# A hybrid decoder layer: decay rows masked on GpSimd, weights and sums loaded in another order, the causal mask as fp32r tiles

## The chip, the cores and the metric

One core of one Trainium2 chip runs the whole program. The metric is the device time of one execution in microseconds (us). The engines are named as the profile names them: PE is TensorE's matmul, PEld its weight load, DVE is VectorE, ACT is ScalarE, POOL is GpSimd, SP issues most of the DMAs.

## The reference

One decoder layer on 1024 tokens of width 1024, all in float32. One projection of the normed input feeds two groups of heads: a differential attention of 4 heads and a gated delta rule of 4 heads, whose outputs are put side by side, projected, and added to the input; an MLP with a squared ReLU of width 4096 follows.

```python
h = rms_norm(x, norm1_w[l])
proj = h @ w_in[l]
...
# group A, per block of 128 queries
s = jnp.where(causal, s, jnp.finfo(jnp.float32).min)
p = jax.nn.softmax(s, axis=-1)
a = p[:, :, 0] - lam * p[:, :, 1]
...
# group B, in chunks of 64
decay = jnp.where(tri, jnp.exp(jnp.where(tri, gdiff, 0.0)), 0.0)
Lmat = jnp.where(strict, jnp.einsum('bhncd,bhnjd->bhncj', k_beta, k) * decay, 0.0)
qk = jnp.where(tri, jnp.einsum('bhncd,bhnjd->bhncj', q, k) * decay, 0.0)
...
x = x + mix @ w_out[l]
h = rms_norm(x, norm2_w[l])
x = x + jnp.square(jax.nn.relu(h @ w_up[l])) @ w_down[l]
```

## The kernel before, in words

Every large product is made of three matmuls: an operand is split into a part rounded to fp32r (suffix H, a cast on ACT) and the rest (suffix L, a subtraction on DVE), and H*H, H*L and L*H are added up in PSUM. So each block of weights goes DMA, ACT cast, DVE subtraction, PE. `load_unit` (L182) does it for the projections, with `wraw` for the raw block and `wH`, `wL` for the parts; `split` (L1298) does it for the MLP.

The kernel has these stages, in order of time:

- **Norm and first columns** (L333 to L390; the order on PE, DVE and ACT is written by hand). For each tile of 128 tokens the input is squared on ACT, scaled on DVE into `hn` (`z_norm`, L328), transposed on PE (L235) and multiplied with two blocks of columns, whose halves `z_round` and `z_rest` make.
- **The delta group's projection** (L512 to L676; the order on all engines comes from a scheduler). `dn_units` makes six blocks of 256 columns, each in four half heads of 24 matmuls into one of two PSUM banks (`ps_dn`). ACT copies the bank to `cp` (L525), and ACT and DVE run a convolution (`cy`, L527 to L529) and make keys, queries and values. `keys` and `queries` transpose them (`ps_t`), multiply them with each other (`ps_m`), and multiply the product with a decay matrix (L633, L656). The decay of head h lies in `dts[h]` (tile `dtm`, 128x1024): `decay_rows` (L576) fills it with the mask `after` (0 where a later token looks at an earlier one, -1e30 elsewhere), which a DMA on SP's queue spreads from SBUF over the eight blocks of the row (L578), and adds the running sums `cgr_d` with a second DMA on GpSimd's queue that accumulates (L579). `decay` (L581) then takes the exponential on ACT (L585). A small inverse (`invert`, L596) runs on DVE beside it, and results are parked in DRAM (`park`, L549).
- **Scan, attention and output projection** (L698 to L1441). PE's order is written by a planner, `Interleave`: streams of work hand it their next piece with a due time worked out from estimated durations, and it takes the first stream, by priority, whose due time has come. `horner` (L712) finishes the inverse, `scan` (L764) runs over 8 chunks with the state `St`, `da_units` (L918) makes the other projection (`ps_qk`), `leave` norms it and `da_turns` (L891) transposes it (`ps_qkt`), `scores` (L1022) makes softmax maps, `values` (L1101) their products, `outproj` (L1200) the output projection and the second norm (`norm2`, L1224). The causal mask of a diagonal block is added by a matmul of a bf16 identity with a bf16 mask (L1079). DVE, ACT, POOL and SP are ordered by the scheduler.
- **MLP** (L1442 to L1725). Up and down projections each take seven products of blocks for eight (sums and differences of operands, as in Strassen's scheme). `down` (L1661) takes two halves of operands, splits them (`split4`), runs 96 matmuls into four PSUM banks, and adds these to the sums `accs`, which come back from DRAM by `load_acc` (L1653). `both` (L1703) makes the differences of weights on DVE, 128x2048 at a time. On PE the order is that of the code, on the other engines the scheduler's.

DMAs on SP's queue are issued in order; each issue that waits holds those behind it.

Of the kernel before, what the change touches and what calls it, by code (L numbers as in the profile page):

```python
# [18 lines left out]
P = 128  # L19
# [97 lines left out]
def tile_hymba_layer(  # L117
# [215 lines left out]
    with tc.manual_schedule(engines={T.engine, V.engine, S.engine}):  # L333
# [47 lines left out]
        z_norm(2)  # L381
        z_gate(0, 1, banks0[1])
        for tb in range(1, NT):
            for u in range(2):
# [3 lines left out]
                if u == 0 and tb + 1 < NT:  # L388
# [5 lines left out]
    identb = const.tile([P, P], BF16, name="identb")  # L394
    V.tensor_copy(identb, ident)
# [3 lines left out]
    caus_f = n1.tile([P, P], F32, name="caus_f")  # L399
    G.memset(caus_f, 0.0)  # L400
    G.affine_select(caus_f, caus_f, pattern=[[-1, P]], compare_op=ALU.is_ge, fill=-1.0e30,
                    base=0, channel_multiplier=1)
    caus = const.tile([P, P], BF16, name="caus")
    V.tensor_copy(caus, caus_f)
# [52 lines left out]
    u, au, e, w1, lw, d1, z1 = (n32(n) for n in ("gu", "gau", "gte", "gw1", "glw", "gd1", "gz1"))  # L457
    V.tensor_tensor(hc(u), av, dtb.unsqueeze(2).broadcast_to([P, 4, 8]), ALU.add)
    V.scalar_tensor_tensor(au, u, -1.0, u, ALU.mult, ALU.max)
    S.activation(e, au, AF.Exp, scale=-1.0)  # L460
# [87 lines left out]

    def park(h, hf, slot, src):  # L549
        nc.sync.dma_start(park_d[h, 4 * hf:4 * hf + 4, :, slot, :].rearrange("c p d -> p c d"), v4(src))  # L550
# [25 lines left out]
    def decay_rows(h):  # L576
        dts[h] = sa.tile([P, SEQ], F32, tag="dtm", name="dtm", bufs=4)
        nc.sync.dma_start(v4(dts[h]), after.unsqueeze(1).broadcast_to([P, NT, P]))  # L578
        G.dma_start(dts[h], cgr_d[h * SEQ:(h + 1) * SEQ].partition_broadcast(P), accum_op=ALU.add)  # L579
# [7 lines left out]
    for h in range(HEADS):  # L587
        decay_rows(h)
# [80 lines left out]
    for n, (kind, h, hf, o) in enumerate(skew(dn_units())):  # L669
        (queries, keys, values_in)[kind](h, hf, o)  # L670
        for _ in range(0 if n < 12 else 2 if n < 16 else 4):
            next(inverse, None)
        if n == 22:
            first_w = load_unit(w_in_v, [(512, 256), (0, 256)], 0, 4, eng=V, rp=sf)
    for _ in inverse:
        pass  # L676

# [15 lines left out]
    sd = sdctx.enter_context(tc.tile_pool(name="sd", bufs=1, **right))  # L693
    px = qctx.enter_context(tc.tile_pool(name="px", bufs=2, space=PSUM, **right))
# [17 lines left out]
    def horner():  # L712
# [13 lines left out]
        at = [flow.now + 5000] * HEADS  # L726
# [164 lines left out]
    def da_turns():  # L891
        for i in range(4 * NT):
# [3 lines left out]
            r = yield from flow.bank("px", at=max(t + 500, qa_free[i % 2] - 500))  # L896
# [21 lines left out]
    def da_units():  # L918
# [5 lines left out]
        w = [(first_w, [0.0] * 4), half_w(w_in_v, todo[0], 4)]  # L924
# [97 lines left out]
    def scores():  # L1022
# [6 lines left out]
        for u, (h, tb) in enumerate(order):  # L1029
# [34 lines left out]
            for m in range(2):  # L1064
# [7 lines left out]
                for pc in range(npc):  # L1072
# [5 lines left out]
                    if last:  # L1078
                        T.matmul(sc[:, 512 * pc + pl - P:512 * pc + pl], identb, caus, start=False, stop=True)  # L1079
# [120 lines left out]
    def outproj():  # L1200
# [23 lines left out]
        def norm2(tb, pos):  # L1224
# [10 lines left out]
            for i in range(2):  # L1235
                sl = slice(512 * i, 512 * i + 512)
                if i == 0 or pos >= 4:
                    normed_by[:] = [V.scalar_tensor_tensor(hn[i], accs[tb][:, sl], r, w2b[:, sl], ALU.mult, ALU.mult)]
                else:
                    S.activation(hn[i], accs[tb][:, sl], AF.Copy, scale=r)  # L1240
                    G.tensor_tensor(hn[i], hn[i], w2b[:, sl], ALU.mult)
            t = flow.chain(act(512, True), act(512, True), vec(1), vec(1), powr(1))
            if pos >= 4:
                return hn, flow.chain(vec(512, 60), vec(512, 60), start=t - flow.HOP)
            flow.chain(vec(512, 60), start=t - flow.HOP)
            t = flow.chain(act(512), ("G", 1230.0), start=t - flow.HOP)
            return hn, t
# [170 lines left out]
    def read_first():  # L1418
        a0 = pools["uz"].tile([P, 2, 512], F32, tag="ua0", name="ua0")
        S.copy(a0, banks["X0"])  # L1420
        V.tensor_tensor(a0, a0, banks["Y"], ALU.add)
        act2(a0)
        nc.sync.dma_start(ud[1][0], a0)
        u[0] = {"a": a0}

# [90 lines left out]
    held(1, [0, 1])  # L1516
    held(2, [0, 1])
# [3 lines left out]
    held(1, [2])  # L1521
    rest(0, 5)
    held(1, [3])
    read_first()
# [95 lines left out]
    bankA = [X[0][:, 0], X[0][:, 1]] + Z  # L1620
# [32 lines left out]
    def load_acc():  # L1653
# [102 lines left out]
```

## Time and profile before

| | us |
|---|---|
| median of 3 runs | 1261.04 (1260.59 to 1262.15) |
| the profiled execution | 1260.75 |
| its span, first to last instruction | 1259.0 |
| PE busy | 1226.7 |
| DVE busy | 834.3 |
| ACT busy | 614.9 |
| POOL busy | 147.1 |
| mean granted clock of TensorE | 0.996 |

A row of the view by group has the line, the engine, the operation, out<-in and the shapes, the count, then the busy time and the mean of one in ns, then the engine's idle time ahead of these instructions and what ended it. In the timeline a row has start, duration, engine, line, operation and count; idle time ahead of it stands in brackets with what ended it. The view by windows gives the busy time of PE, PEld, DVE, ACT and POOL in a stretch, the granted clock, and the busy share and rate of the DMA engines. Times count from the span's start.

### The profile page before, as it was taken

What the parts mean: (1) busy time and instruction counts of PE and PEld (TensorE: products, weight loads), DVE (VectorE), ACT (ScalarE), POOL (GpSimd) and SP (SyncE); (2) the same over time, 40 slices, a digit from 0 to 9 for tenths busy, and PEclk for the clock granted to TensorE, in tenths of its full rate; (3) what the DMA queues carried; (4) which work ended last, traced back from release to release, by engine and by line L of the source; (5) the groups of instructions that cost most, each with busy time, mean ns of one, the idle gap of its engine ahead of it and who ended that gap; (6) DMA issues with size and microseconds to landing.
All of it is one profiled execution on the core that took longest, in us unless ns stands there. A gap on an engine that the chain in (4) does not pass through costs nothing.

```text
span 1259.0 us, 17761 instructions
## 1 busy us (share of the span) xinstructions
PE 1226.7 (97%) x6338; PEld 1027.0 (82%) x6338; DVE 834.3 (66%) x1425; ACT 614.9 (49%) x1216; POOL 147.1 (12%) x185
## 2 busy tenths in 40 slices
PE   8997999999899999999999999999999999999998
PEld 7985888887777887888878888888888788888887
DVE  5555879558877658765799555665566865687553
ACT  5347555424456545645667444454563333333331
POOL 1111210113442132202310000000000000000000
PEclk9999999999999999999999999999999999999999
DMA  7176551457665657333446534534368755422301
GB/s 254 50 181 177 148 146 54 116 158 232 192 196 150 204 181 234 94 85 97 167 135 208 199 142 154 184 138 147 118 235 320 297 200 200 167 101 100 132 36 67
DMA packets 164655, 201.27 MB, mean 160 GB/s; under 512 B 20608, under 2 KB 124376, under 8 KB 164568
## 3 DMA queue, kind: packets, MB, share of 16 engines
q1 hardware_dynamic: 163992, 198.05, 47.9%
q0 software_dynamic: 576, 2.10, 0.8%
q8 instruction: 50, 0.82, 0.3%
q14 instruction: 37, 0.30, 0.1%
HBM read 132.45 MB, written 65.55 MB: 157 GB/s over the span
## 4 chain that ended last, share of the span: by engine, by line
PE 83%; DMA 6%; DVE 5%; ACT 2%; issue 2%; SPq 1%; POOL 1%; DVEq 0%; POOLq 0%; ACTq 0%
PE X L1382 4%; PE X L1381 4%; PE X L1383 4%; PE X L1678 3%; PE X L1679 3%; PE X L1677 3%; PE ps_dn L202 3%; PE ps_dn L203 3%; PE ps_dn L204 3%; PE ps_qk L943 3%; PE ps_qk L945 3%; PE ps_qk L944 3%; PE Y L1382 2%; PE Y L1381 2%; PE Y L1383 2%; PE ps_o L1127 2%
## 5 line engine op out<-in xcount | busy, mean ns | idle before, releaser
L1300 ACT CAST hH<-ur 128x1024 fp32r<-128x1024 f32 x56 | 58.5, 1049 | 175.7 <-PE Z L1678 85.2
L1301 DVE TENSOR_TENSOR hL<-ur,hH 128x1024 fp32r<-128x1024 f32 x56 | 68.4, 1224 | 83.3 <-ACT hH L1300 83.2
L1301 DVE TENSOR_TENSOR op<-raw,op 128x1024 fp32r<-128x1024 f32 x48 | 58.7, 1224 | 74.8 <-PE X L1382 40.9
L1678 PE MATMUL X<-hL,hH 128*128 128x512 f32 x224 | 87.6, 391 | 2.8 <-DVE hL L1301 2.8
L1677 PE MATMUL X<-hH 128*128 128x512 f32 x224 | 87.5, 391 | 1.4 <-DVE b L1579 1.4
L1679 PE MATMUL X<-hH,hL 128*128 128x512 f32 x224 | 87.3, 390 | 0.0
L202 PE MATMUL ps_dn<-hH,wH 128*128 128x512 f32 x192 | 76.5, 399 | 6.9 <-ACT cp L525 5.8
L943 PE MATMUL ps_qk<-wH,hH 128*128 128x512 f32 x192 | 82.1, 428 | 0.2 <-ACT wH L196 0.2
L203 PE MATMUL ps_dn<-hL,wH 128*128 128x512 f32 x192 | 76.4, 398 | 0.0
L944 PE MATMUL ps_qk<-wL,hH 128*128 128x512 f32 x192 | 75.5, 393 | 0.5 <-DVE wL L197 0.4
L945 PE MATMUL ps_qk<-wH,hL 128*128 128x512 f32 x192 | 75.9, 395 | 0.0
L204 PE MATMUL ps_dn<-hH,wL 128*128 128x512 f32 x192 | 75.8, 396 | 0.0
L1301 DVE TENSOR_TENSOR hL<-dw,hH 128x1024 fp32r<-128x1024 f32 x56 | 68.1, 1220 | 2.6 <-ACT hH L1300 2.6
L1300 ACT CAST op<-raw 128x1024 fp32r<-128x1024 f32 x48 | 50.3, 1051 | 35.0 <-PE Y L1383 19.9
L1300 ACT CAST hH<-dw 128x1024 fp32r<-128x1024 f32 x56 | 58.4, 1047 | 14.8 <-PE Z L1679 8.0
L529 DVE SCALAR_TENSOR_TENSOR cy<-cp,pv,cy 128x512 f32<-128x512 f32 x72 | 53.8, 749 | 10.5 <-ACT cy L527 10.0
L1085 ACT ACTIVATE pexp<-ps_sc,mx 128x128 f32<-128x128 f32 (+7 forms) x64 | 47.3, 741 | 24.3 <-DVE mx L1081 24.1
L196 ACT CAST wH<-wraw 128x512 fp32r<-128x512 f32 x64 | 37.3, 622 | 35.8 <-DMA wraw<-in_w_in_dram 24.8
L1081 DVE TENSOR_REDUCE mx<-ps_sc 128x1 f32<-128x128 f32 (+7 forms) x64 | 47.0, 754 | 10.8 <-PE ps_sc L1079 10.4
L1212 PE MATMUL ps_op<-wH,hH 128*128 128x512 f32 x128 | 54.0, 422 | 0.0
L1678 PEld LDWEIGHTS X<-hL,hH 128*128 128x128 f32 x224 | 42.2, 188 | 12.0 <-DVE hL L1301 3.2
L1677 PEld LDWEIGHTS X<-hH 128*128 128x128 f32 x224 | 42.3, 189 | 10.5 <-DVE b L1579 1.8
(358 smaller groups left out, 3445.7 us busy)
## 6 DMA issues: line engine op xcount, KB each, us to landing
ur<-ud SPq DMA_DIRECT2D x28, 1024.0 KB, 4.9
raw<-in_w_up_dram SPq DMA_DIRECT2D x32, 512.0 KB, 3.7
dw<-in_w_down_dram SPq DMA_DIRECT2D x32, 512.0 KB, 7.1
qk_d<-qa SPq DMA_DIRECT2D x32, 256.0 KB, 3.0
ud<-ua SPq DMA_DIRECT2D x16, 512.0 KB, 4.0
ud<-s SPq DMA_DIRECT2D x16, 512.0 KB, 2.6
wraw<-in_w_in_dram SPq DMA_DIRECT2D x24, 256.0 KB, 5.1
wraw<-in_w_in_dram SPq DMA_DIRECT2D x48, 128.0 KB, 2.7
```

Source lines behind the costliest of these rows:

```text
L202: T.matmul(ps, lh(k), rh(k), start=(k == 0), stop=False)
L203: T.matmul(ps, lh(k), rl(k), start=False, stop=False)
L204: T.matmul(ps, ll(k), rh(k), start=False, stop=(k == n - 1))
L943: T.matmul(ps, hH[:, 4 * kh + k, sl], wh[:, k, :], start=(kh + k == 0), stop=False)
L944: T.matmul(ps, hH[:, 4 * kh + k, sl], wl[:, k, :], start=False, stop=False)
L945: T.matmul(ps, hL[:, 4 * kh + k, sl], wh[:, k, :], start=False, stop=(kh + k == 4))
L1300: S.copy(dst[0], src)
L1301: V.tensor_tensor(dst[1], src, dst[0].bitcast(F32), ALU.subtract)
L1381: T.matmul(ps, op[0][:, k, cs], h[0][:, k, :], start=start and k == 0, stop=False, skip_group_check=True)
L1677: T.matmul(bank[t], v[0][:, j, sl], v[2][:, j], start=s0, stop=False, skip_group_check=True)
L1678: T.matmul(bank[t], v[0][:, j, sl], v[3][:, j], start=False, stop=False, skip_group_check=True)
L1679: T.matmul(bank[t], v[1][:, j, sl], v[2][:, j], start=False, stop=s1, skip_group_check=True)
```

## The change

The edits are these. (1) `z_norm(2)` is emitted after two of the four roundings of the second block and no longer after all. (2) The bf16 identity and mask of L394 to L404 go; fp32r tiles `identr` and `caus` are made at the start of the attention's pools, and the mask's matmul uses them. (3) `decay_rows` loads the running sums by a plain broadcast on SP's queue and adds the mask with one GpSimd instruction; heads 0 and 1 are made at the start, heads 2 and 3 after the fifth and the seventh half head, behind the last parked block. (4) The second half of `first_w`, the first weights of `da_units`, is loaded before the attention's stage. (5) In the planner `horner`'s first due time goes from 5000 to 8000 ns after the start, the transposes of `da_turns` are due 2000 in place of 500 ns after their estimate, and `norm2` counts 1800 ns for the power on GpSimd. (6) `norm2` makes all halves on DVE. (7) `read_first` is cut in three pieces that stand between the `held` steps. (8) In `down` bank A begins with the Z banks, the first half of all goes over two token tiles at a time, the differences of weights are made in quarters inside `split4`, and `load_acc` is cut in two around the weights "d". A tile (`au`) of the gate's arithmetic goes, its value is written to `e` itself.

```diff
--- before.py
+++ after.py
@@ -378,7 +378,8 @@
             z_rest(1, i)
-        z_norm(2)
+            if i == 1:
+                z_norm(2)
         z_gate(0, 1, banks0[1])
@@ -391,17 +392,9 @@
     V.memset(ones, 1.0)
-    identb = const.tile([P, P], BF16, name="identb")
-    V.tensor_copy(identb, ident)
     tri = sp.tile([P, P], F32, name="tri")
...
                     base=0, channel_multiplier=-1)
-    caus_f = n1.tile([P, P], F32, name="caus_f")
-    G.memset(caus_f, 0.0)
-    G.affine_select(caus_f, caus_f, pattern=[[-1, P]], compare_op=ALU.is_ge, fill=-1.0e30,
-                    base=0, channel_multiplier=1)
-    caus = const.tile([P, P], BF16, name="caus")
-    V.tensor_copy(caus, caus_f)
 
@@ -454,10 +447,10 @@
     n32 = lambda name: sp.tile([P, 32], F32, name=name)
-    u, au, e, w1, lw, d1, z1 = (n32(n) for n in ("gu", "gau", "gte", "gw1", "glw", "gd1", "gz1"))
+    u, e, w1, lw, d1, z1 = (n32(n) for n in ("gu", "gte", "gw1", "glw", "gd1", "gz1"))
     V.tensor_tensor(hc(u), av, dtb.unsqueeze(2).broadcast_to([P, 4, 8]), ALU.add)
-    V.scalar_tensor_tensor(au, u, -1.0, u, ALU.mult, ALU.max)
-    S.activation(e, au, AF.Exp, scale=-1.0)
+    V.scalar_tensor_tensor(e, u, -1.0, u, ALU.mult, ALU.max)
+    S.activation(e, e, AF.Exp, scale=-1.0)
     V.tensor_scalar(w1, e, 1.0, None, ALU.add)
@@ -546,8 +539,10 @@
 
+    parked = []
+
     def park(h, hf, slot, src):
-        nc.sync.dma_start(park_d[h, 4 * hf:4 * hf + 4, :, slot, :].rearrange("c p d -> p c d"), v4(src))
+        parked.append(nc.sync.dma_start(park_d[h, 4 * hf:4 * hf + 4, :, slot, :].rearrange("c p d -> p c d"), v4(src)))
 
@@ -575,8 +570,8 @@
         dts[h] = sa.tile([P, SEQ], F32, tag="dtm", name="dtm", bufs=4)
-        nc.sync.dma_start(v4(dts[h]), after.unsqueeze(1).broadcast_to([P, NT, P]))
-        G.dma_start(dts[h], cgr_d[h * SEQ:(h + 1) * SEQ].partition_broadcast(P), accum_op=ALU.add)
+        nc.sync.dma_start(dts[h], cgr_d[h * SEQ:(h + 1) * SEQ].partition_broadcast(P))
+        G.tensor_tensor(v4(dts[h]), v4(dts[h]), after.unsqueeze(1).broadcast_to([P, NT, P]), ALU.add)
 
@@ -584,7 +579,7 @@
 
-    for h in range(HEADS):
+    for h in range(2):
         decay_rows(h)
@@ -670,10 +665,14 @@
             next(inverse, None)
+        if n in (4, 6):
+            with tc.issue_after(parked[-1].ins):
+                decay_rows(n // 2)
         if n == 22:
-            first_w = load_unit(w_in_v, [(512, 256), (0, 256)], 0, 4, eng=V, rp=sf)
+            first_w = [load_unit(w_in_v, [(512, 256), (0, 256)], 0, 4, eng=V, rp=sf)]
     for _ in inverse:
         pass
+    first_w.append(load_unit(w_in_v, [(512, 256), (0, 256)], 4, 4, eng=V, rp=sf))
 
@@ -691,6 +690,14 @@
     sd = sdctx.enter_context(tc.tile_pool(name="sd", bufs=1, **right))
+    identr = ap.tile([P, P], F32R, name="identr")
+    V.tensor_copy(identr, ident)
+    caus_f = ap.tile([P, P], F32, tag="om", name="om", bufs=2)
+    G.memset(caus_f, 0.0)
+    G.affine_select(caus_f, caus_f, pattern=[[-1, P]], compare_op=ALU.is_ge, fill=-1.0e30,
+                    base=0, channel_multiplier=1)
+    caus = ap.tile([P, P], F32R, name="caus")
+    V.tensor_copy(caus, caus_f)
     px = qctx.enter_context(tc.tile_pool(name="px", bufs=2, space=PSUM, **right))
@@ -723,7 +730,7 @@
         loads(0)
-        at = [flow.now + 5000] * HEADS
+        at = [flow.now + 8000] * HEADS
         for hf in range(2):
@@ -893,7 +900,7 @@
             g, kind, tb, qn, t = late[0]
-            r = yield from flow.bank("px", at=max(t + 500, qa_free[i % 2] - 500))
+            r = yield from flow.bank("px", at=max(t + 2000, qa_free[i % 2] - 500))
             late.pop(0)
@@ -921,7 +928,7 @@
 
-        w = [(first_w, [0.0] * 4), half_w(w_in_v, todo[0], 4)]
+        w = [(w, [0.0] * 4) for w in first_w]
         freed = [0.0, 0.0]
@@ -1076,7 +1083,7 @@
                     if last:
-                        T.matmul(sc[:, 512 * pc + pl - P:512 * pc + pl], identb, caus, start=False, stop=True)
+                        T.matmul(sc[:, 512 * pc + pl - P:512 * pc + pl], identr, caus, start=False, stop=True)
                 scv = sc.rearrange("p (a b) -> p a b", b=512)[:, :npc, :pl]
@@ -1234,17 +1241,9 @@
                 sl = slice(512 * i, 512 * i + 512)
-                if i == 0 or pos >= 4:
-                    normed_by[:] = [V.scalar_tensor_tensor(hn[i], accs[tb][:, sl], r, w2b[:, sl], ALU.mult, ALU.mult)]
-                else:
-                    S.activation(hn[i], accs[tb][:, sl], AF.Copy, scale=r)
-                    G.tensor_tensor(hn[i], hn[i], w2b[:, sl], ALU.mult)
-            t = flow.chain(act(512, True), act(512, True), vec(1), vec(1), powr(1))
-            if pos >= 4:
-                return hn, flow.chain(vec(512, 60), vec(512, 60), start=t - flow.HOP)
-            flow.chain(vec(512, 60), start=t - flow.HOP)
-            t = flow.chain(act(512), ("G", 1230.0), start=t - flow.HOP)
-            return hn, t
+                normed_by[:] = [V.scalar_tensor_tensor(hn[i], accs[tb][:, sl], r, w2b[:, sl], ALU.mult, ALU.mult)]
+            t = flow.chain(act(512, True), act(512, True), vec(1), vec(1), ("G", 1800.0))
+            return hn, flow.chain(vec(512, 60), vec(512, 60), start=t - flow.HOP)
 
@@ -1418,10 +1417,13 @@
         S.copy(a0, banks["X0"])
+        yield
         V.tensor_tensor(a0, a0, banks["Y"], ALU.add)
+        yield
         act2(a0)
...
         u[0] = {"a": a0}
+        yield
 
@@ -1514,14 +1516,17 @@
     held(1, [0, 1])
+    first = read_first()
+    next(first)
     held(2, [0, 1])
...
     held(1, [2])
+    next(first)
     rest(0, 5)
     held(1, [3])
-    read_first()
+    next(first)
     combine(0, 6)
@@ -1617,7 +1622,7 @@
     ur = ctx.enter_context(tc.tile_pool(name="ur", bufs=1, **right))
-    bankA = [X[0][:, 0], X[0][:, 1]] + Z
+    bankA = Z + [X[0][:, 0], X[0][:, 1]]
     bankB = [X[1][:, 0], X[1][:, 1], Y[:, 0], Y[:, 1]]
@@ -1650,15 +1655,18 @@
 
-    def load_acc():
-        for tb in tiles:
+    def load_acc(tbs):
+        for tb in tbs:
             nc.sync.dma_start(accs[tb], acc_d[tb])
 
-    def split4(dst, src):
+    def split4(dst, src, made=None):
         for j in (0, 2):
-            split([x[:, j:j + 2] for x in dst], src[:, j:j + 2])
-
-    def down(kg, wd, i, flip, n, out, start, stop):
+            js = slice(j, j + 2)
+            if made:
+                V.tensor_tensor(src[:, js], made[0][:, js], made[1][:, js], ALU.subtract)
+            split([x[:, js] for x in dst], src[:, js])
+
+    def down(kg, wd, i, flip, n, out, start, stop, made=None):
         bank = bankB if flip ^ (kg % 2) else bankA
@@ -1667,9 +1675,10 @@
             split4(v[0:2], raw)
-            split4(v[2:4], wd[n][s])
+            split4(v[2:4], wd[n][s], made and [wd[x][s] for x in made])
             u_raw(m + 4 if m else 1)
             seq = [(j, t) for t in range(4) for j in range(4)] if final and s else \
+                [(j, t) for ts in ((0, 1), (2, 3)) for j in range(4) for t in ts] if m == 0 else \
                 [(j, t) for j in range(4) for t in range(4)]
@@ -1693,31 +1702,25 @@
     with tc.issue_after(last.ins):
-        load_acc()
-        for n in "dc":
-            for s in range(2):
-                dn_raw(0, n, s)
+        load_acc(tiles[:4])
+        for s in range(2):
+            dn_raw(0, "d", s)
+        load_acc(tiles[4:])
+        for s in range(2):
+            dn_raw(0, "c", s)
     for kg in range(NK):
...
 
-        def both(dst, l, r):
-            for s in range(2):
-                V.tensor_tensor(wd[dst][s], wd[l][s], wd[r][s], ALU.subtract)
-
         down(kg, wd, 1, 0, "a", (0, lo), True, False)
-        both("b", "b", "a")
-        down(kg, wd, 5, 1, "b", (1, hi), True, False)
-        both("b", "d", "b")
-        down(kg, wd, 6, 0, "b", (0, hi), False, False)
+        down(kg, wd, 5, 1, "b", (1, hi), True, False, "ba")
+        down(kg, wd, 6, 0, "b", (0, hi), False, False, "db")
         down(kg, wd, 3, 1, "d", (0, hi), False, True)
-        both("a", "b", "a")
-        down(kg, wd, 7, 0, "a", (1, hi), False, False)
+        down(kg, wd, 7, 0, "a", (1, hi), False, False, "ba")
         down(kg, wd, 2, 1, "c", (0, lo), True, True)
...
                 dn_raw(kg + 1, "a", s)
-        both("b", "c", "b")
-        down(kg, wd, 4, 0, "b", (1, lo), False, True)
+        down(kg, wd, 4, 0, "b", (1, lo), False, True, "cb")
         if kg + 1 < NK:
```

The scheduler's orders move with it. On SP, at the place where the running sums are written (`cgr_d`) and the decay rows `dtm` are filled; `wraw` are raw weights, `park_d` parked keys. Before:

```order
L480 DMA cgr_d<-cgr 32x128
L194 DMA wraw<-in_w_in_dram 128x2x256
L578 DMA dtm<-after 128x8x128 x4
L194 DMA wraw<-in_w_in_dram 128x2x256 x6
L550 DMA park_d<-k_1040 128x4x128
```

and now:

```order
L473 DMA cgr_d<-cgr 32x128
L194 DMA wraw<-in_w_in_dram 128x2x256 x3
L573 DMA dtm<-cgr_d 128x1024 x2
L194 DMA wraw<-in_w_in_dram 128x2x256 x5
L545 DMA park_d<-k_1024 128x4x128
```

The four mask broadcasts are gone, and two blocks of weights stand ahead of the two broadcasts that remain.

On ACT, in the same stage, from the cast of the second block's weights (`wH_1263`, now `wH_1247`) on; `dtm` is the decay's exponential and `cp` the copy that frees a PSUM bank. Before:

```order
L196 CAST wH_1263<-wraw 128x512 x3
L536 ACTIVATE cth<-cy 128x512
L525 COPY cp<-ps_dn 128x512
L527 ACTIVATE cy<-cp,pv 128x512
L536 ACTIVATE cth<-cy 128x512
L196 CAST wH_1263<-wraw 128x512
L196 CAST wH_1538<-wraw 128x512
L536 ACTIVATE cth<-cy 128x512
L525 COPY cp<-ps_dn 128x512
L585 ACTIVATE dtm<-dtm,ncg 128x128 x4
```

and now:

```order
L196 CAST wH_1247<-wraw 128x512 x4
L529 ACTIVATE cth<-cy 128x512
L518 COPY cp<-ps_dn 128x512
L520 ACTIVATE cy<-cp,pv 128x512
L580 ACTIVATE dtm<-dtm,ncg 128x128 x7
L529 ACTIVATE cth<-cy 128x512
L580 ACTIVATE dtm<-dtm,ncg 128x128 x7
L518 COPY cp<-ps_dn 128x512
L529 ACTIVATE cth<-cy 128x512
L580 ACTIVATE dtm<-dtm,ncg 128x128 x2
```

Fourteen exponentials now stand ahead of the fourth copy of a bank, and no cast of weights of the third block does.

On DVE, in the down projection's first products; `dw` are weights, `ur` activations, `hL` a rest, `acc` a sum. Before, from the first difference of the weights "d":

```order
L1705 TENSOR_TENSOR dw<-dw 128x2048
L1301 TENSOR_TENSOR hL<-ur_7666,hH 128x2x512
L1705 TENSOR_TENSOR dw<-dw 128x2048 x2
L1301 TENSOR_TENSOR hL<-dw,hH 128x2x512 x2
L1684 TENSOR_TENSOR acc<-acc,X_7473 128x512 x2
```

and now:

```order
L1666 TENSOR_TENSOR dw<-dw 128x1024 x3
L1300 TENSOR_TENSOR hL<-dw,hH 128x2x512
L1666 TENSOR_TENSOR dw<-dw 128x1024 x2
L1300 TENSOR_TENSOR hL<-ur_9528,hH 128x2x512
L1666 TENSOR_TENSOR dw<-dw 128x1024
L1300 TENSOR_TENSOR hL<-dw,hH 128x2x512
```

The differences are half as long, and the first rest of the new operand stands behind three of them, 3072 columns in place of 6144.

## The prediction

> **What bounds the kernel now.** I read the page's busy shares first, then the view by windows, then PE's waits.
>
> ```profile
> span 1259.0 us, 17761 instructions
> PE 1226.7 (97%) x6338; PEld 1027.0 (82%) x6338; DVE 834.3 (66%) x1425; ACT 614.9 (49%) x1216; POOL 147.1 (12%) x185
> 90.00:120.00 30.00, 22.74 (x109) 17.69 (x109) 12.66 (x32) 19.40 (x69) 2.85 (x4) 0.94 0.80 209
> 290.00:335.00 45.00, 38.84 (x237) 33.56 (x236) 38.26 (x97) 19.93 (x53) 20.39 (x19) 0.96 0.68 217
> 940.00:1000.00 60.00, 55.87 (x239) 45.42 (x238) 43.46 (x37) 22.82 (x24) 0.00 (x0) 0.97 0.91 342
> ```
>
> PE sets the time. It is idle for 1259.0 − 1226.7 = 32 us, and the change takes none of its matmuls away. So an edit is worth what it takes from PE's waits, and beside that the stretches in which the granted clock falls. The three windows hold both: the lost clock is 30 × 0.06, 45 × 0.04 and 60 × 0.03, each time 1.8 us. The longest waits, PE's side first:
>
> ```profile
> PE ps_dn L202 <- ACT cp L525: 5.8, 2, 4.6
> PE ps_qkt L899 <- DVE qn L986: 3.0, 1, 3.0
> PE X L1678 <- DVE hL L1301: 2.8, 1, 2.8
> PE ps_qkt L899 <- DVE qa L906: 1.8, 1, 1.8
> PE ps_tr L235 <- DVE hn L249: 1.5, 1, 1.5
> PE X L1677 <- DVE b L1579: 1.4, 1, 1.4
> PE ps_dn L202 <- ACT wH L196: 1.0, 1, 1.0
> PE ps_A L798 <- DVE sr L790: 1.0, 1, 1.0
> PE ps_qk L944 <- DVE wL L197: 0.4, 1, 0.4
> ```
>
> Each wait is a single event, or two. One clock loss belongs to the 4.6, one to the 3.0 and one to the 2.8: these are the only waits above 2 us, and each lies in one of the windows.
>
> **The decay rows.** Here is where the 5.8 (a wait of 4.6 and one of 1.2) and the 1.0 come from: PE's rows, ACT's, SP's, then transfers (count, size, median us from issue to landing).
>
> ```profile
> 102.86 0.79 PE L202 MATMUL ps_dn<-hH,wH 128*128 128x512 f32 x1 [4.60 <-ACT cp L525]
> 95.66 0.62 ACT L196 CAST wH<-wraw 128x512 fp32r<-128x512 f32 x1 [8.59 <-DMA wraw<-in_w_in_dram]
> 101.18 0.62 ACT L196 CAST wH<-wraw 128x512 fp32r<-128x512 f32 x1 [4.90 <-DMA wraw<-in_w_in_dram]
> 109.21 3.64 ACT L585 ACTIVATE dtm<-dtm,ncg 128x128 f32<-128x128 f32 x12
> 77.50 0.33 SPq L480 DMA_DIRECT2D cgr_d<-cgr  x1
> 78.41 4.83 SPq L578 DMA_DIRECT2D dtm<-after  x4
> dtm<-after SPq DMA_DIRECT2D x4, 512.0 KB, 5.7
> dtm<-cgr_d POOLq DMA_DIRECT2D x4, 512.0 KB, 10.6
> fsx_d<-lt SPq DMA_DIRECT2D x32, 16.0 KB, 1.5
> ```
>
> Four issues of 4.83 us stand on SP ahead of raw weights, and eight transfers of 512 KB share the engines with them. ACT stands twice for `wraw` (8.59 and 4.90 us); behind the second cast comes the copy that frees PE's bank. After the change two transfers of 512 KB are left at this place, behind two more blocks of weights. I take the casts' waits off the path: 5.8 + 1.0 + 1.8 of clock = 8.6 us.
>
> What is late next? Fourteen exponentials are ahead of the fourth copy of a bank, and the copy behind them is what PE needs. The sums are issued at 77.50 and land 1.5 later, at 79.0 (a 16 KB transfer's time); a broadcast takes some 5.7 and its issue 4.83 ÷ 4 = 1.2, so the two land at 84.7 and 85.9. Two additions of 128x1024 on POOL follow, an operation that the trace doesn't have. From the rows below, 128x256 takes 0.645 us and 128x512 1.336; 1.336 + 2 × 0.691 = 2.7 is my estimate. The rows are ready at 87.4 and 90.1. Fourteen exponentials at 3.64 ÷ 12 = 0.30 take 4.2, a `cth` and the copy 0.6 each: the bank is free at 95.5 if all stood behind the second addition. PE's product before it ends at 102.86 − 4.60 = 98.3, less the 1.0 taken off: 97.3. That is 1.8 us of cover. If the broadcast took the 10.6 of the accumulating one, the copy would come 4.9 − 1.8 = 3.1 late.
>
> I keep the smaller wait, 1.2, since ACT's backlog of exponentials ahead of the copy (12 of them at 109.21) only moves, and add 0.5 for DVE held up by POOL. Sum: 8.6 − 1.2 − 0.5 = **6.9 us off**. Bounds: 8.6 off, and 6.9 − 3.1 = 3.8 off. The rows of heads 2 and 3 are filled later, behind parked blocks; their exponentials come after those of heads 0 and 1, so they have that cover, and without it they would cost the same 3.1.
>
> The extra cost of POOL is seen in these rows: two groups on POOL, a row of DVE, and the same DVE instruction's extremes (min/median/max in ns).
>
> ```profile
> L980 POOL TENSOR_TENSOR qsq<-qn 128x256 f32<-128x256 f32 x32 | 20.6, 645 | 67.7 <-ACT qn L970 40.8 <-ACT qn L965 16.7 <-DVE sn L981 10.2
> L831 POOL TENSOR_TENSOR zgt<-zgt,dnwb 128x512 f32<-128x512 f32 x8 | 10.7, 1336 | 20.0 <-DMA zgt<-zg_d 20.0
> 318.34 1.86 DVE L986 TENSOR_TENSOR qn<-qn,rn 128x256 f32<-128x256 f32 x2
> 318.56 1.36 POOL L831 TENSOR_TENSOR zgt<-zgt,dnwb 128x512 f32<-128x512 f32 x1 [0.25 <-DMA zgt<-zg_d]
> L986 DVE TENSOR_TENSOR qn<-qn,rn x32: 408/426/1517, 251.8 to 474.9; 128x256 f32<-128x256 f32 x32
> ```
>
> While POOL's multiplication ran, the pair on DVE took 1.86 us in place of 2 × 0.426: DVE stood for about 1 us, the length of what was left of POOL's instruction. Four additions of 2.7 could hold DVE for 10.8 us. DVE is 12.66 of 30 us busy at this place, and PE waits for ACT and not for DVE, so I charge 0.5 only; the full price is a rival.
>
> The Trainium skill (page "SBUF — State Buffer", section "Who interferes with whom") states the harder rule: a DVE instruction with two inputs in SBUF and a GpSimd instruction that reads SBUF exclude each other, and the second to issue fully blocks. The 1517 against 426 ns agrees. By the rule alone the sum would carry 10.8 in place of 0.5.
>
> **The prologue.** PE waits 1.5 for `hn` (DVE, L249), whose square on ACT stands behind four casts:
>
> ```profile
> 16.80 2.21 ACT L317 CAST wH<-wraw 128x520 fp32r<-128x520 f32 x4
> ```
>
> Two casts fewer ahead are 2.21 ÷ 2 = **1.1 us off**; bounds 0 (the other casts then are late) and 1.5 (the whole wait).
>
> **The first weights.** The 0.4 wait for `wL` goes, since the second half is loaded a stage earlier: **0.4 off**.
>
> **The planner.** The transposes of `da_turns` wait once 1.8 for `qa` and once 3.0 for `qn`. Asked 1.5 us later (2000 for 500), PE takes other work first: 3.0 off, and the 3.0 falls to 1.5, below every wait at which the clock fell, so 1.8 of clock goes too. `horner`, due 3 us later, and the new order will leave a wait somewhere; I put it at 1.0, that of L798. **3.8 off**. Bounds: 4.8 + 1.8 = 6.6 off with both waits gone and none new; 3.0 on, if all of `horner`'s 3 us became waiting and no clock came back.
>
> **The down projection.** The new bank order takes PE's wait for `b` (1.4), as the Z banks have been read earlier. The 2.8 comes from this:
>
> ```profile
> 959.83 9.03 SPq L1655 DMA_DIRECT2D acc<-acc_d  x8
> 982.84 2.29 DVE L1705 TENSOR_TENSOR dw<-dw 128x2048 f32<-128x2048 f32 x1 [2.73 <-DMA dw<-in_w_down_dram]
> 986.19 4.49 DVE L1705 TENSOR_TENSOR dw<-dw 128x2048 f32<-128x2048 f32 x2
> 990.59 2.35 DVE L1301 TENSOR_TENSOR hL<-dw,hH 128x1024 fp32r<-128x1024 f32 x2
> 991.86 0.50 PE L1678 MATMUL X<-hL,hH 128*128 128x512 f32 x1 [2.76 <-DVE hL L1301]
> ```
>
> PE stops at 991.86 − 2.76 = 989.1. With weights "d" as late as now, three quarters of 2.29 ÷ 2 and one rest of 2.35 ÷ 2 would end at 982.84 + 3.4 + 1.2 = 987.4, still ahead of it; half of the 9.03 of issues moves behind "d", which gives up to 4.5 more. So both waits and the clock go: 1.4 + 2.8 + 1.8 = **6.0 off**. If the smaller wait stays in another place, 4.6.
>
> **The mask's matmul.** Sixty-four of them (4 heads, 2 maps, 8 diagonal blocks), bf16 before:
>
> ```profile
> 382.53 0.40 PE L1077 MATMUL ps_sc<-KS,qb 128*128 128x512 f32 x1
> 382.77 0.23 PE L1079 MATMUL ps_sc<-caus,identb 128*128 128x128 bf16 x1
> 382.81 0.48 PE L943 MATMUL ps_qk<-wH,hH 128*128 128x512 f32 x1
> 383.13 0.39 PE L944 MATMUL ps_qk<-wL,hH 128*128 128x512 f32 x1
> 421.79 0.27 PE L1077 MATMUL ps_sc<-KS,qb 128*128 128x128 f32 x1
> 421.91 0.23 PE L1079 MATMUL ps_sc<-caus,identb 128*128 128x128 bf16 x1
> ```
>
> From its start to the next is 0.04 us, but the next holds PE 0.32 in place of the 0.23 of the pair before: 0.13 in all. An fp32r matmul of 128 columns takes 0.12 (421.79 to 421.91). So I charge **nothing**. If the 0.09 isn't due to the bf16 matmul and stays, it is 64 × 0.08 = 5 us on; the other bound is 0.4 off.
>
> **The rest.** The second norm's halves on DVE, `read_first` in pieces, the gate's tile: **nothing**. No wait of PE names them; DVE, 66% busy, takes four more halves and loses POOL's hold. Bounds ±1.
>
> **The sum** against the profiled execution of 1260.75 (span 1259.0 and 1.75 around it): −1.1 − 6.9 − 0.4 − 3.8 − 6.0 = −18.2, hence 1242.55. The median of the runs is 0.3 above the profiled one: **1243**.
>
> **The rivals.**
> - *The planner gives it back.* An order made from estimates moves its waits: if the stage of 290 to 335 keeps its waits and clock loss and `horner` is 3.0 late, the planner's term is +3.0 and not −3.8: 1250. For it: DVE is 38.26 of 45 us busy there, so what comes later may still come too late. Against: PE has the filler of L943 and L1076 there.
> - *POOL holds DVE on the path.* If each of the four additions stops DVE for its 2.7 us and PE for as long, 10.8 − 0.5 = 10.3 comes on: 1253. For it: 1517 against 426 ns. Against: PE waits for ACT's copies, and DVE idles over half of that stage. This is the case by the Trainium skill's rule named above.
> - Both together: 1260, no change to be told.
> - *Patience starves PE (slower).* The turns of `da_turns` feed the scores. If PE has no other work to put in their place, then half of the 32 turns of L899 (the other half under cover) cost 1.5 us each: 24 us on, 1267. It decides from the point at which the projection's matmuls run out. Against: at 382.8 the projection's L943 still stands between scores.
>
> **How the numbers follow.** Forecast 0.56; the planner 0.20; POOL 0.13; both 0.06; starving 0.05. The terms' best ends add to −1.5 − 8.6 − 0.4 − 6.6 − 6.0 − 0.4 − 1 = −24.5, hence 1236.5 and the low end of 1236; the high end takes in the first two rivals: 1254. The forecast's own range is 1237 to 1247. Faster by over 0.2% (2.5 us, about what a measurement can tell from no change) is 0.56 + 0.20 + 0.13 = 0.89; within 0.06; slower 0.05.
>
> **What would show it.** After: no wait for `wraw` on ACT near 95 and 101, no PE wait over 2 us at L202, clock 1.00 in the first window: the decay step is right. Waits of 2 us and more of L202 for `cp`, with additions of `dtm` on POOL ahead of them or DVE instructions stretched by 2 us beside them, would show the second rival. A PE wait at L899 above 2 us or a clock below 0.98 in 290 to 335 shows the first. PE's wait at L1678 under 0.5 us and a clock of 1.00 in the third window show the down step. A spacing of 0.12 at the mask's matmul with the next at 0.23 shows that step; 0.32 still after it would put 5 us on. Gaps of PE between 380 and 470 that add up to 10 us or more would make the whole forecast wrong.

## The result, and the profile after

The changed kernel takes 1244.85 us (1243.05 to 1245.71), the kernel before 1260.82 beside it: a ratio of 0.9871, 95% interval 0.9854 to 0.9888. The forecast was 1243, its range 1236 to 1254. The profiled execution took 1245.71, 15.0 less than the one of before. Taken step by step, the gain is not the forecast's sum.

The page's first rows after, and the view by windows (us, then PE, PEld, DVE, ACT, POOL busy, granted clock):

```profile
span 1244.0 us, 17734 instructions
PE 1220.2 (98%) x6338; PEld 1032.5 (83%) x6338; DVE 844.0 (68%) x1445; ACT 611.0 (49%) x1212; POOL 146.3 (12%) x181
90.00:120.00 30.00, 28.33 (x155) 24.11 (x153) 27.52 (x66) 20.81 (x76) 8.31 (x9) 1.00 0.46 126
290.00:335.00 45.00, 42.35 (x258) 36.60 (x258) 38.68 (x100) 22.91 (x63) 19.57 (x20) 1.00 0.74 230
940.00:1000.00 60.00, 60.00 (x267) 49.69 (x266) 49.52 (x48) 22.53 (x23) 0.00 (x0) 1.00 0.88 335
```

The clock stands at 1.00 in all three windows: the three losses of 1.8 us are gone. PE's idle time in them falls from 7.3, 6.2 and 4.1 us to 1.7, 2.7 and 0. To see what each step gave, I read four points on PE's timeline: the start of the last matmul of the first columns, of the last one of the projection, of the first one into the MLP's Z banks, and of the last one of all. Before:

```profile
65.49 0.28 PE L304 MATMUL ps_z<-wH,hL 128*128 128x260 f32 x1
231.82 0.39 PE L204 MATMUL ps_dn<-hH,wL 128*128 128x512 f32 x1
655.21 0.39 PE L1381 MATMUL Z<-hH,wH 128*128 128x512 f32 x1
1254.28 0.39 PE L1679 MATMUL Y<-hH,hL 128*128 128x512 f32 x1
```

and after:

```profile
65.52 0.28 PE L304 MATMUL ps_z<-wH,hL 128*128 128x260 f32 x1
223.54 0.39 PE L204 MATMUL ps_dn<-hH,wL 128*128 128x512 f32 x1
646.59 0.39 PE L1380 MATMUL Z<-hH,wH 128*128 128x512 f32 x1
1239.33 0.39 PE L1688 MATMUL Y<-hH,hL 128*128 128x512 f32 x1
```

| step | forecast, us | by these starts, us | undone on the chip, us |
|---|---|---|---|
| prologue | −1.1 | 0.0 | |
| decay rows | −6.9 | −8.3 | +7.7 |
| first weights, planner (and mask, norm, `read_first`) | −4.2 | −0.3 | +6.1; the due times alone +16.2 |
| down projection | −6.0 | −6.3 | +5.7 |
| sum | −18.2 | −14.9 | |

The last column is the median of a kernel with that step undone, less 1244.85 (for the third row the due times and the first weights alone). So two steps came as forecast or better, and the planner's gain is the one that is short.

How short is known only roughly. Six kernels below (e1, e2, e4, e9, e11, e12) have the same code from the projection's end to the MLP; in their profiles this stage takes 421.0 to 423.7 us, after 423.05, before 423.4. So its gain lies between none and 2.4 us, against 4.2 forecast. The kernel before has one profile only. PE's waits between the projection and the MLP, after (total, times, longest):

```profile
PE ps_tr L235 <- DMA mt<-mixa_d: 2.7, 2, 1.4
PE ps_sc L1083 <- ACT pexp L1092: 2.5, 3, 1.2
PE ps_A L793 <- DVE S L822: 1.7, 2, 1.5
PE ps_sc L1084 <- DMA qb<-qk_d: 1.6, 2, 1.2
```

The waits at L899 (now L906) of 3.0 and 1.8 are gone, and no wait of this stage is above 1.5. But many small ones took their place. Windows over the same stage, first before, then after:

```profile
232.00:360.00 128.00, 121.13 (x842) 104.19 (x841) 90.16 (x225) 54.42 (x148) 42.63 (x42) 0.99 0.61 184
360.00:480.00 120.00, 117.48 (x636) 95.84 (x636) 81.28 (x204) 69.64 (x184) 35.89 (x45) 1.00 0.63 190
480.00:640.00 160.00, 157.73 (x931) 132.39 (x930) 112.42 (x241) 98.25 (x255) 33.95 (x42) 1.00 0.43 134
```

```profile
224.00:360.00 136.00, 130.07 (x896) 112.20 (x895) 93.44 (x240) 59.67 (x167) 48.22 (x50) 1.00 0.59 179
360.00:480.00 120.00, 115.41 (x629) 97.56 (x628) 83.54 (x202) 69.06 (x178) 35.75 (x43) 1.00 0.64 194
480.00:632.00 152.00, 148.29 (x880) 128.76 (x880) 105.98 (x233) 88.64 (x239) 26.11 (x36) 1.00 0.41 128
```

PE idles 6.9 + 2.5 + 2.3 = 11.7 us before and 5.9 + 4.6 + 3.7 = 14.2 after. One us is won up to 360 and 3.5 are lost behind it; the clock's 1.8 pays for that. So what the edits take from the old waits comes back as new ones, and the experiments ask by what.

### The profile page after: what moved, and what is told of

Same layout as the page of the kernel before. It is cut to its first block, busy times and chain, and to the rows that moved or that the text cites. A ratio compares the mean times of both kernels' runs of the same rounds, so it can differ in the third digit from the quotient of the medians.

```text
span 1244.0 us, 17734 instructions
## 1 busy us (share of the span) xinstructions
PE 1220.2 (98%) x6338; PEld 1032.5 (83%) x6338; DVE 844.0 (68%) x1445; ACT 611.0 (49%) x1212; POOL 146.3 (12%) x181
## 4 chain that ended last, share of the span: by engine, by line
PE 84%; DVE 5%; DMA 5%; POOL 2%; ACT 2%; issue 2%; SPq 1%; DVEq 0%; POOLq 0%; ACTq 0%
PE X L1382 5%; PE X L1381 5%; PE X L1380 5%; PE X L1686 4%; PE X L1687 4%; PE X L1688 4%; PE ps_dn L204 3%; PE ps_dn L202 3%; PE ps_dn L203 3%; PE Y L1382 2%; PE Y L1381 2%; PE Y L1380 2%; PE Y L1686 2%; PE Z L1686 2%; PE Z L1687 2%; PE Y L1687 2%
## 5 line engine op out<-in xcount | busy, mean ns | idle before, releaser
L522 DVE SCALAR_TENSOR_TENSOR cy<-cp,pv,cy 128x512 f32<-128x512 f32 x72 | 61.6, 858 | 6.6 <-ACT cy L520 6.0
L1088 DVE TENSOR_REDUCE mx<-ps_sc 128x1 f32<-128x128 f32 (+7 forms) x64 | 47.3, 753 | 12.4 <-PE ps_sc L1086 11.8
L1221 PE MATMUL ps_op<-wH,hL 128*128 128x512 f32 x128 | 50.3, 393 | 0.0
L1220 PE MATMUL ps_op<-wL,hH 128*128 128x512 f32 x128 | 50.0, 390 | 0.0
L1380 PE MATMUL Y<-hH,op 128*128 128x512 f32 x128 | 49.8, 389 | 0.0
```

Source lines behind the costliest of these rows:

```text
L1380: T.matmul(ps, op[0][:, k, cs], h[0][:, k, :], start=start and k == 0, stop=False, skip_group_check=True)
```

## The experiments

Every kernel was timed beside the kernel before, on the same chip, and its ratio is to that one. The kernel before spreads more than the changed one: beside the experiments it took 1258.2 to 1270.2 us (medians 1261.9 to 1264.7), where the first timing gave 1260.82. So I compare medians with the changed kernel's 1244.85, and those of e10, e11 and e12 with its second timing beside them, 1245.2 (e9). A difference of 1 or 2 us between timings is not told apart.

**The decay rows as before (e1).**

```diff
-        nc.sync.dma_start(dts[h], cgr_d[...].partition_broadcast(P))
-        G.tensor_tensor(v4(dts[h]), v4(dts[h]), after..., ALU.add)
+        nc.sync.dma_start(v4(dts[h]), after...)
+        G.dma_start(dts[h], cgr_d[...].partition_broadcast(P), accum_op=ALU.add)
...
+    for h in range(HEADS):
```

> The changed kernel (1244.9) with the decay rows filled as before: mask broadcast on SP's queue, accumulating transfer on GpSimd's, all four heads at the start. If the decay step is worth what the trace after shows (the projection stage ends 8.3 us earlier), the time is 1253, with L202 waiting some 4 us for cp, ACT waiting for wraw near 95 and 101 us and one clock loss. If only the waits of the prediction's sum count (6.9), it is 1252. If the casts' waits come from the order of the weights and not from the four extra transfers, it stays within 2 us of 1245.

1252.52 (1252.04 to 1253.78), ratio 0.9911 (0.9882 to 0.9939): 7.7 more. Its waits:

```profile
PE ps_dn L202 <- ACT cp L518: 5.8, 2, 4.6
PE ps_dn L202 <- ACT wH L196: 1.0, 1, 1.0
```

They are those of before to a tenth, and the projection takes 166.3 us as before (158.0 after). So the way in which the rows are filled causes these waits, and the whole of the projection's gain hangs on it. Whether fewer transfers or fewer heads at the start count more was not split.

This run says something of the planner too. All other edits are in it, and its projection is as long as before:

```profile
233.07 0.39 PE L204 MATMUL ps_dn<-hH,wL 128*128 128x512 f32 x1
654.53 0.39 PE L1377 MATMUL Z<-hH,wH 128*128 128x512 f32 x1
```

The stage between takes 421.5 us, 1.9 less than before, and PE idles 12.4 us in it, as it did before (12.4). So most of the planner's gain is missing even where the projection was not shortened.

**The mask's additions on DVE (e2).** In `decay_rows`, `G.tensor_tensor` becomes `V.tensor_tensor`.

> The changed kernel with the mask's four additions on DVE in place of GpSimd. After shows two additions of 2.8 us on POOL at 86.4, four DVE instructions at 86.3 that take 7.13 us in place of 3.0, and a PE wait of 1.67 us for k. If POOL holds DVE (the second rival's mechanism), two additions of about 1.1 us on DVE cost less than the 4.1 us of hold: DVE's instructions beside them are back at 0.75 us, the wait of 1.67 shrinks to under 0.5, and the time is 1243 to 1244. If DVE is late for another reason, the wait stays at 1.5 or grows by DVE's 2.2 us of more work and the time is 1245 to 1247.

1244.08 (1242.08 to 1245.15), ratio 0.9841 (0.9811 to 0.9870). The total can't be told from the change's; the trace can. After, DVE, POOL and PE; then, of e2, all 72 of the DVE instruction (min/median/max in ns), DVE's own addition, and PE at the same place:

```profile
86.30 7.13 DVE L522 SCALAR_TENSOR_TENSOR cy<-cp,pv,cy 128x512 f32<-128x512 f32 x4
86.42 5.66 POOL L574 TENSOR_TENSOR dtm<-dtm,after 128x1024 f32<-128x1024 f32 x2 [30.12 <-DMA dtm<-cgr_d]
94.08 0.66 PE L559 MATMUL ps_t<-ident,k 128*128 128x128 f32 x4 [1.67 <-DVE k L531]
```

```profile
L522 DVE SCALAR_TENSOR_TENSOR cy<-cp,pv,cy x72: 726/749/753, 79.4 to 227.2; 128x512 f32<-128x512 f32 x72
L574 DVE TENSOR_TENSOR dtm<-dtm,after x4: 1217/1222/1226, 86.7 to 132.2; 128x1024 f32<-128x1024 f32 x4
94.92 0.49 PE L559 MATMUL ps_t<-ident,k 128*128 128x128 f32 x3
```

Four instructions of 0.75 took 7.13 us while POOL added; with the additions on DVE none takes above 0.753, and PE's wait is gone. So POOL's additions do hold DVE: by 4.1 us here, of which 1.67 reach PE. The projection ends 1.6 us earlier than after, though its first columns ended 0.4 later in that execution.

**Both due times as before (e3)**, `flow.now + 5000` and `t + 500`.

> The changed kernel with the planner's two due times of before (horner 5000 for 8000, the transposes of da_turns 500 for 2000). By the prediction's sum these are worth 3.8 us: 1248.7, with the two waits at L899 (1.8 and 3.0) and a clock loss back. By the trace after, where the stage from the end of the projection to the MLP takes only some 0.4 us less than before although its clock loss and both waits are gone, they are worth nothing in the sum: 1244 to 1246, and what comes back at 290 to 335 us goes away again at 360 to 610. If they cost time (the rival's side), it is 1241 to 1243.

1261.0 (1256.96 to 1264.75), ratio 0.9978 (0.9959 to 0.9998): 16 us more than the change. None of the three expectations came true: neither 3.8, nor nothing, nor a loss. So the two due times were taken apart.

**Horner's due time alone as before (e5), da_turns' alone (e6).**

> The changed kernel with horner's first due time alone as before (5000 for 8000). With both due times as before it took 1261.0, 16 us more than the change, and PE waited some 5 us for gb (transfers of horner's operands) at 231 to 259 us. If these waits are the cause, this kernel has them and takes 5 to 8 us more than the change: 1250 to 1253. If the cause is the turns of da_turns, it stays at 1244 to 1247.

> The changed kernel with the patience of da_turns alone as before (500 for 2000). If the waits for the transposes' operands (1.4 and 2.4 us, and one clock loss, in the kernel with both due times as before) are the cause, it takes 5 to 8 us more than the change: 1250 to 1253, with these waits. By the prediction's sum (the waits of 1.8 and 3.0 and the clock) it is 4.8 more: 1249.7. If the cause is horner's due time, it stays at 1244 to 1247.

e5 took 1261.55 (1259.19 to 1266.36), ratio 0.9996 (0.9978 to 1.0014); e6 1246.53 (1244.61 to 1247.11), ratio 0.9868 (0.9844 to 0.9893). Horner's 3 us carry all of it, over twice what I expected of e5. The patience of `da_turns`, on which I had put most of the planner's term, gives 1.7 us by the medians, and the interval of e6's ratio covers the change's: nothing that can be told. Yet in e6 PE waits again at L906 for `qn`, 4.1 us in all and once 2.7; the clock stays at 1.00, and the stage to the MLP takes 422.0 us. The old waits are back and the time is not. In e5 PE waits for:

```profile
PE ps_p L739 <- DMA gb<-fsg_d: 4.3, 4, 2.5
PE ps_sc L1083 <- DMA qa<-qk_d: 2.6, 2, 2.0
```

Horner begins before its operands `gb` have landed. These waits are only a part: the stage takes 440.0 us for the 423.05 after; PE idles 23.9 us in it for 14.2, and it is busy 416.1 for 408.6, with three clock losses (one of them 0.91 granted from 240 to 260 us). That the projection, displaced by horner, makes `qa` late for the scores is how I read the rest; it was not taken apart.

**Both due times new in the kernel before (e7), and both old with the first weights loaded late in the changed one (e8).** The diff is e8's; e7 makes the reverse of its last two edits in the kernel before.

```diff
-    first_w.append(load_unit(w_in_v, ..., 4, 4, eng=V, rp=sf))
-        w = [(w, [0.0] * 4) for w in first_w]
+        w = [(first_w[0], [0.0] * 4), half_w(w_in_v, todo[0], 4)]
-        at = [flow.now + 8000] * HEADS
+        at = [flow.now + 5000] * HEADS
-            r = yield from flow.bank("px", at=max(t + 2000, qa_free[i % 2] - 500))
+            r = yield from flow.bank("px", at=max(t + 500, qa_free[i % 2] - 500))
```

> The kernel before with the planner's two due times alone new (8000 and 2000). By the prediction's sum it takes 3.8 us less than before. If the due times only mend what another part of the change costs (the norm on DVE, the weights loaded ahead), it is within 1.5 us of before. If they are worth the 16 us that they are worth in the changed kernel, it is 16 less.

> The changed kernel with both due times as before and the second half of the first weights loaded in the attention's stage as before. If the due times were needed because these weights now stand ahead of gb on SP's queue, the waits for gb go and the time is 1246 to 1250. If not, it stays at 1258 to 1263 as with the due times alone.

e7 took 1272.13 (1271.02 to 1273.67), ratio 1.0075 (1.0050 to 1.0100): slower than before. e8 took 1250.97 (1249.84 to 1253.06), ratio 0.9908 (0.9882 to 0.9934), one us above what I expected if the early weights make `gb` late. In the changed kernel with old due times, the earlier weights cost 1261.0 − 1251.0 = 10 us; in the kernel before, with its late weights, the new due times cost 9.5 (0.0075 of 1262); both together win 6.1 in the changed kernel. New due times with late weights in the changed kernel were not run. In e8, PE's two longest waits, and SP's issues ahead of them (then those of before):

```profile
PE ps_qk L949 <- ACT wH L196: 3.7, 1, 3.7
PE ps_qkt L905 <- DVE qn L992: 3.0, 1, 3.0
```

```profile
221.94 0.33 SPq L603 DMA_DIRECT2D fsg_d<-fg  x1
225.66 3.17 SPq L729 DMA_DIRECT2D gb<-fsg_d  x7
...
229.40 4.34 SPq L729 DMA_DIRECT2D gb<-fsg_d  x9
233.83 0.38 SPq L194 DMA_DIRECT2D wraw<-in_w_in_dram  x1
```

```profile
226.19 0.45 SPq L608 DMA_DIRECT2D fsg_d<-fg  x1
230.44 1.27 SPq L723 DMA_DIRECT2D gb<-fsg_d  x3
...
239.19 1.80 SPq L194 DMA_DIRECT2D wraw<-in_w_in_dram  x4
```

This is a link that the forecast lacked. In e8 the projection ends 7.6 us earlier than before, but the inverse's result `fg`, written to DRAM and read back as `gb`, comes only 4.2 us earlier (221.94 for 226.19), and the weights, issued behind 16 loads of `gb`, 5.4 (233.83 for 239.19). So in the shorter kernel the wait for weights that was 0.2 and 0.4 us is 3.7, with a clock loss behind it (0.83 granted from 225 to 245 us).

Weights loaded early take this wait away, but then `gb` is late. In e5 `fg` leaves at 221.52, 0.4 earlier than in e8, and still `gb` follows more slowly:

```profile
226.38 0.33 SPq L730 DMA_DIRECT2D gb<-fsg_d  x1
228.55 0.36 SPq L545 DMA_DIRECT2D park_d<-kn  x1
228.96 3.40 SPq L730 DMA_DIRECT2D gb<-fsg_d  x7
```

In e8 seven loads go out from 225.66 on, and PE never waits for `gb`. In e5 the first load stands 2.1 us for POOL, which clears `gb` only when DVE is done with the early weights, and the next seven stand behind a parked block. Horner's due time, later by 3 us, steps over that. `fg` itself is late in both: its last link on DVE ends 2.6 us after the link ahead of it (0.45 before), since two `cy` stand ahead of its parts. This is read from the traces; no run undoes it.

**The down projection as before (e4), and its loads alone (e11).**

```diff
-        load_acc(tiles[:4])
+        load_acc(tiles)
         for s in range(2):
             dn_raw(0, "d", s)
-        load_acc(tiles[4:])
```

This is e11; e4 also has the old bank order, the old order of token tiles, and differences of 2048 columns in one piece.

> The changed kernel with the down projection as before (bank order, order of sums and weights, differences of 128x2048 in one piece). By the prediction's sum and by the trace after (6.0 and 6.3 us) the time is 1251, with PE's waits of 1.4 for b and 2.8 for hL and one clock loss. If an earlier edit had already taken these waits away, it stays within 1.5 us of 1245.

> The changed kernel with the order of loads of before in the down projection: all eight sums ahead of the weights d; bank order and differences in quarters stay. By the prediction's working the quarters alone suffice (the rest that PE needs ends 1.7 us ahead of PE's stop): the time is that of the changed kernel, and PE doesn't wait at L1686. If it is the load order that takes the wait away, PE waits 2 to 3 us for hL there, the clock falls, and the time is 3 to 5 us more.

e4 took 1250.57 (1248.22 to 1252.74), ratio 0.9888 (0.9850 to 0.9926), with the two waits back and one clock loss:

```profile
PE X L1686 <- DVE hL L1300: 4.2, 1, 4.2
PE X L1685 <- DVE b L1584: 1.4, 1, 1.4
```

e11 took 1243.88 (1242.95 to 1245.56), ratio 0.9840 (0.9814 to 0.9866), no more than the change beside it (1245.2), and PE doesn't wait in the down projection. The order of loads isn't needed; what is left of the step, pieces of 1024 columns and the orders of banks and token tiles, does the work. Among these no run decides.

**The mask as bf16 (e10)**, the two tiles `identr` and `caus` with BF16 in place of F32R, and the change once more (e9).

> The changed kernel itself, as the measure for the three beside it: 1243 to 1246, ratio to the kernel before 0.987.

> The changed kernel with mask and identity as bf16 tiles again. By the spacing in the two traces (before the mask's matmul, the one ahead of it and the one behind it take 0.466 us together, after 0.448, 64 times) this kernel takes 1.1 us more than the changed one beside it. By the prediction it is within 0.4 us. If the fp32r weights cost time (the upper bound of the prediction), it takes up to 5 us less.

e9 took 1245.2 (1243.81 to 1245.56), ratio 0.9847 (0.9822 to 0.9873); e10 1245.54 (1243.03 to 1247.75), ratio 0.9854 (0.9827 to 0.9881). The total can't tell them apart. One place in the trace after:

```profile
373.95 0.23 PE L1086 MATMUL ps_sc<-caus,identr 128*128 128x128 f32 x1
374.01 0.45 PE L1083 MATMUL ps_sc<-KS,qa 128*128 128x512 f32 x1
374.30 0.40 PE L1084 MATMUL ps_sc<-KS,qb 128*128 128x512 f32 x1
```

The mask's own start-to-start is 0.06, the next 0.29. Over the places without a wait, from the start of the matmul ahead to that behind the next one, it is 0.466 us on the mean before, 0.448 after and 0.457 in e10. Against e10, the only kernel that differs in the type alone, fp32r gains 0.009 us in each of 64 places, 0.6 us; the other 0.6 to the kernel before lies in what stands beside them.

**Two edits more (e12):** the mask on DVE as in e2, and in the prologue:

```diff
             if i == 1:
                 z_norm(2)
-        z_gate(0, 1, banks0[1])
+                z_gate(0, 1, banks0[1])
```

> The changed kernel with two more edits: the mask's additions on DVE, and in the prologue the gate of tile 0 ahead of the last two roundings. If POOL's hold of DVE is the whole of the wait of 1.67 for k, and DVE's two last rests ahead of the gate are the whole of the wait of 0.56 at L302, both waits go: 2.2 us less than the changed kernel beside it. If the planner's stage answers by waits of its own, the gain at the end of the projection stays at 2.2 and less of it is left at the end.

1242.54 (1240.0 to 1244.47), ratio 0.9824 (0.9797 to 0.9851), 2.7 less than e9; the two ratios' intervals overlap, so likely faster, not settled. Both waits are gone, and the projection ends 1.9 us earlier than after; the prologue's wait that went, in the trace after:

```profile
21.75 1.30 DVE L321 TENSOR_TENSOR wL<-wraw,wH 128x520 fp32r<-128x520 f32 x2
23.30 0.15 DVE L313 COPY ab<-ps_z 128x8 f32<-128x8 f32 x1
23.59 0.36 PE L302 MATMUL ps_z<-wH,hH 128*128 128x260 f32 x1 [0.56 <-DVE ab L313]
```

## Why the prediction was right, and where it wasn't

**The decay step** was right in its mechanism and under-sized: 8.3 in place of 6.9. In the projection PE's idle time falls from 7.3 to 1.7 us and its busy time from 159.0 to 156.3. The idle time should have fallen by 5.1: the 1.2 that I kept for ACT's backlog went too, as the bank was copied in time, and a wait of 0.4 for `lt` (L571) with it; what came back is POOL's hold, 1.67 for the 0.5 charged. The busy time should have fallen by the clock's 1.8 and fell by 2.7; what the rest is was not taken apart. Of the chain that I worked out, the additions took 2.8 us (2.7), but the broadcasts 7.7 (5.7), so the second row was ready at 92.1 for the 90.1. The copy was done at 94.5 for the 95.5 all the same, because seven of the fourteen exponentials stood behind the first addition alone. So the cover held partly by luck.

**POOL's hold**, the second rival: its mechanism is there and its price isn't. POOL stops DVE for 4.1 us at the first two additions and for another 4.0 at the other two, and the 10.3 needed PE to stand for all of it. The Trainium skill's rule (page "SBUF — State Buffer", section "Who interferes with whom") names the pair rightly. Of the 8.1 us only 1.67 reached PE, and DVE's slack took the rest.

**The planner and the first weights** are where the sum failed: 4.2 forecast, 0.3 found in the profiled execution and none to 2.4 in the others. The step that failed is the one that read each edit's worth from the waits of before. The waits at L899 and the clock loss did go, but PE idles in the stage for as long as before: 12.4 us before, 14.2 after, 13.2 in e9. The shorter projection is not needed for that, since e1 idles 12.4 too. The 3.8 was put on the patience of the turns, and e6 brings these waits back at a cost of 1.7 us or nothing; horner's due time, which I had taken for a cost, decides over 16 us once the weights are early. The 0.4 for the early weights was the wait of a projection that ended at 231.8; behind the shorter one it is 3.7 and a clock loss. So these two edits keep 6.1 us from being lost rather than win 4.2.

The first rival (the planner gives it back) named the outcome better, but not the way: the clock and the waits at L899 did go, and the time came back at 360 to 640 as waits of 0.1 to 1.5 us. What makes each of these was not taken apart. "Patience starves PE" is refuted for the changed kernel; in the kernel before, both new due times together do cost 9.5, and the waits there are for late operands.

**The down step** was right: 6.3 for 6.0. The working said that the quarters suffice without the new order of loads, and e11 shows it.

**The prologue** gained its 1.1 at the place named (the wait for `hn` fell from 1.49 to 0.38), but DVE's part of the gate (L313) then stood behind two rests of weights: 0.56 came back at once, unforeseen. The remaining 0.5 can't be seen in the starts. The kernels with this prologue end the first columns anywhere from 64.99 to 66.92 us (before: 65.49), and in the execution shown the matmuls ahead had ended 0.6 later than before: from 10.2 to 11.7 us PE began 5 of them, before 8.

**The mask and the rest**: nothing, within what the times can tell.

That the total came within 2 us of the forecast is in part luck: errors of opposite sign, 1.4 and 0.3 more than forecast on the decay rows and the down step, 3.9 and 1.1 less on the planner and the prologue.

## What to carry to other kernels

A wait in the profile of before is not yet the price of an edit. The stage ahead must keep its length: when one edit shortens it, look at which inputs of the next stage move with it and which hang on another chain, because those turn into the new wait. And in a stage whose order a planner writes, taking one wait away can leave the idle time as it was, so count the idle time of the whole stage, in more than one execution. Edits that step over such a wait (weights loaded early, a later due time) can each cost time alone and win it together, so they have to be costed, and undone, as a group. Here a GpSimd instruction of 2 to 3 us was also a stop for DVE beside it.

## What the runs showed of the hardware that I had not expected

POOL's additions of 128x1024 and the DVE instructions of 0.75 us beside them hold each other. The first two additions took 2.83 us on the mean; a DVE instruction had started 0.12 ahead of the first. The other two began ahead of DVE's and took 2.40. One of those, with the DVE instruction beside it, and then all of DVE's group after (min/median/max in ns):

```profile
125.15 2.40 POOL L574 TENSOR_TENSOR dtm<-dtm,after 128x1024 f32<-128x1024 f32 x1 [5.25 <-DMA dtm<-cgr_d]
125.28 2.81 DVE L522 SCALAR_TENSOR_TENSOR cy<-cp,pv,cy 128x512 f32<-128x512 f32 x1
L522 DVE SCALAR_TENSOR_TENSOR cy<-cp,pv,cy x72: 717/748/2885, 79.0 to 228.8; 128x512 f32<-128x512 f32 x72
```

DVE does the same addition in 1.22 us, about half of POOL's 2.40.

The clock did not follow from the length of a wait alone. A single wait of 2.7 us stands ahead of a clock loss in e10 (0.91 granted from 575 to 595 us), one of 2.7 us cost none in e6 (1.00 from 330 to 350), and in e7 a wait of 1.8 us stands ahead of a loss (0.91 from 415 to 435). That a wait of 1.5 us lies below every one at which the clock had fallen was right for the changed kernel, but it was one trace's finding.
